# Mamba-2 scan of a trunk kernel: one masked 256x256 matrix per head instead of chunk products with a carried state

## The chip, the cores and the metric

The kernel runs on one core of a Trainium2 chip. The metric is the device time of one execution, in microseconds (us). The engines are named as the profile names them: PE (TensorE, its weight loads apart as PEld), DVE (VectorE), ACT (ScalarE), POOL (GpSimd) and SP (SyncE, which issues the transfers).

## The reference, cut to what matters

Two layers of a decoder trunk on 256 tokens of width 1024. Each layer is a gated FFN, a mixer and a second FFN; the mixer of the first layer is latent attention, that of the second is a Mamba-2 SSD block. Six sublayers follow each other, numbered s = 0 to 5; the SSD block is s = 4. Only its scan and the gate behind it are touched. With 32 heads of 64 columns, 4 groups of 8 heads, a state of 128 and two chunks of 128 tokens, the scan is

```python
a_cum = jnp.cumsum(a, axis=-1)                                   # a = dt * A, in each chunk
decay_ls = jnp.exp(jnp.where(causal, a_cum[l] - a_cum[s], -inf))
cb = einsum('bclgn,bcsgn->bcgls', Cc, Bc)
y_diag = einsum('bcgls,bcgkls,bcsgkp->bclgkp', cb, decay_ls, xdt)
states = einsum('bclgn,bcgkl,bclgkp->bcgkpn', Bc, exp(a_cum[-1] - a_cum), xdt)
# prev: the state that is carried from chunk 0 into chunk 1 (zero for chunk 0)
y_off = einsum('bclgn,bcgkpn,bcgkl->bclgkp', Cc, prev, exp(a_cum))
y = y_diag + y_off + d_skip * xs
g = rms_norm over each group of 512 columns of (y * silu(z))     # then g @ w_out
```

With two chunks the carried state can be left out: the part of chunk 1 that comes from chunk 0 is C B^T times exp(sum of a from s to l), a third 128x128 block per head beside the two causal ones on the diagonal. Both forms give the same y.

## The kernel before

Everything is kept transposed: channels on the partitions, the 256 tokens along the free axis. A weight matrix comes from DRAM in pieces of [128, 1024]; each is split into a float32r part (`whi`, a cast on ACT, line 197) and its rest (`wlo`, a subtraction on DVE, line 198), and a product is three float32r passes over them (`mm3`, line 282). One [128 x 1024] by [1024 x 256] projection is 24 such passes and is called PROJ here. Split pieces lie in `W_BUFS` = 5 buffers, and `piece` (line 222) asks for two pieces ahead.

`ssd` (line 1237) runs 41 projections in the order of `SSD_ORDER`: c is a chunk of the convolved channels (B, C and four of x for each group), z one of the gate. Between them it calls `step` (line 1243), which advances two lines of generators by one `yield` each: the scans (`ssd_dt`, then `ssd_group` for the groups 0 to 3) and the gates (`gate`, one for each group, which may run only when the group's scan has ended). There is one step ahead of a projection and one behind it, so two steps lie together between two projections. What a step issues on PE is pinned (line 271): it stays behind what was traced ahead of it. The Tile scheduler places the rest by program order and readiness.

`ssd_group` (line 1115) has 14 parts. For a group it makes, in this order: the products of B and C for the two chunks, and a transpose of B (`cbp`, lines 1171 to 1175); eight transposes that bring x to tokens by channels (`xs_tok`), scaled by dt on DVE (`xs_dt`, line 1135); four times, for two heads each, `decay` (line 1138), a bank with the cumulated decays of the two heads, spread over the partitions by two float32r products with 64 rows, and four bfloat16 products that add the causal mask; `decay_exp` (line 1150), four ACT exponentials; `times_cb` (line 1158), one DVE product with C B^T; and `ymm` (line 1163), four float32 products whose stationary operand is the masked matrix and whose moving operand is 64 columns of x. Beside these stand the state (`xe`, `sp`, `st`), its product with C (`off`), the scaling and the sum on DVE (`yt`), eight transposes back to channels by tokens (`tp`) and four DVE instructions that add the skip term (line 1232).

`gate` (line 1302) multiplies by silu(z) on DVE, squares on ACT, adds the four squares on POOL (line 1313), and leaves the reciprocal root (`rstd_cols`: four PE records of one column, a DVE scaling, a POOL power) for `spread` on PE; then DVE scales (line 1324) and the result is split for the products with w_out. `down` (line 440) makes these: the first `SSD_EARLY` = 4 chunks of the output take their first 12 of 16 terms early, in blocks of 4 terms (12 passes), with one hook behind each block: the last evacuation, 11 steps, and one that runs what is left. The last four terms of those chunks need the gate of group 3. A weight piece holds 8 terms, so an early chunk's second piece stays in its buffer until those last terms are made.

## Time and profile before

| | us |
|---|---|
| median of three runs | 1114.9 |
| lowest and highest of them | 1113.39 and 1115.18 |
| span of the profiled execution | 1112.1 |
| PE busy in it | 1087.2 (98%) |
| DVE busy | 865.9 (78%) |
| ACT busy | 613.1 (55%) |
| POOL busy | 55.1 (5%) |

The profiled execution's span goes from its first to its last instruction; the 2.8 us between it and the median are taken as what lies around it. Times in rows are us from the start of the span, durations in the grouped views ns. A float32 product of the program shows as two PE records, a float32r or bfloat16 product as one, a transpose as one. Records on PE overlap (a product's fill and drain lie beside its neighbours), so what a product costs is read from the distance between starts.

### The profile page before, as it was taken

Reading aid. Unit: us, or ns where it says so; the run is one execution under the profiler, and the core shown is the slowest. Engines: PE = TensorE matmul, PEld = TensorE weight load, DVE = VectorE, ACT = ScalarE, POOL = GpSimd, SP = SyncE. Lnnn points to the kernel's source line nnn. Section 1 sums busy time; section 2 is a strip of 40 time slices with the busy share of each in tenths; the row PEclk is TensorE's granted clock in tenths of the full one; section 3 lists DMA queues with packets and bytes.
Section 4 is the critical chain, followed back from the end, with each engine's and each line's share of the span. In section 5 each row is a group of like instructions: output and inputs, shape, how many; then the busy total and the mean of one; then the engine's idle time right before and its main releaser. Section 6 shows DMA issues by size and latency. Waiting matters only on the chain.

```text
span 1112.1 us, 21992 instructions
## 1 busy us (share of the span) xinstructions
PE 1087.2 (98%) x8950; PEld 1068.5 (96%) x8950; DVE 865.9 (78%) x1534; ACT 613.1 (55%) x1081; POOL 55.1 (5%) x108
## 2 busy tenths in 40 slices
PE   4999999999999999999999999999999899999998
PEld 3999999998999999999999999999999899999998
DVE  5889899789779878766998885697877677766642
ACT  3555444468667544444754444597678456544431
POOL 3000020010000000000000000000200300000000
PEclk9999999999999999999999999999999999999999
DMA  8888998754156888775799995444324254666630
GB/s 346 344 331 323 348 357 319 257 207 163 39 189 229 311 299 302 276 267 204 250 359 347 342 332 196 175 156 148 114 96 152 79 211 169 225 228 228 232 128 20
DMA packets 37401, 258.56 MB, mean 232 GB/s; under 512 B 4274, under 2 KB 5426, under 8 KB 6708
## 3 DMA queue, kind: packets, MB, share of 16 engines
q1 hardware_dynamic: 37300, 257.16, 63.4%
q8 instruction: 70, 1.15, 0.4%
q14 instruction: 31, 0.25, 0.1%
HBM read 256.10 MB, written 1.05 MB: 231 GB/s over the span
## 4 chain that ended last, share of the span: by engine, by line
PE 94%; DVE 2%; DMA 1%; ACT 1%; issue 1%; POOL 1%; SPq 0%; POOLq 0%; ACTq 0%; DVEq 0%
PE bank L272 92%; PE bank L277 2%; DMA raw<-in_adaw_dram 1%; DVE raw L236 1%; DVE wlo L198 0%; POOL t L1313 0%; DVE sl L307 0%; ACT whi L197 0%; ACT t L892 0%; DVE sl L1324 0%; SPq L328 0%; POOL sl L557 0%; POOL rr L415 0%; DVE sl L1232 0%; DVE sl L1306 0%
## 5 line engine op out<-in xcount | busy, mean ns | idle before, releaser
L272 PE MATMUL bank<-sl,whi 128*128 128x256 f32 (+1 forms) x5312 | 954.5, 283 | 4.5 <-ACT whi L197 4.4
L272 PEld LDWEIGHTS bank<-sl,whi 128*128 128x128 f32 x5312 | 816.3, 189 | 7.5 <-ACT whi L197 4.7
L272 PE MATMUL bank<-sl,wlo 128*128 128x256 f32 (+1 forms) x2656 | 747.7, 282 | 6.3 <-DVE wlo L198 6.3
L197 ACT CAST whi<-raw 128x1024 fp32r<-128x1024 f32 (+1 forms) x342 | 354.4, 1040 | 358.1 <-PE bank L272 251.9
L272 PEld LDWEIGHTS bank<-sl,wlo 128*128 128x128 f32 x2656 | 502.8, 189 | 7.0 <-DVE wlo L198 6.8
L198 DVE TENSOR_TENSOR wlo<-raw,whi 128x1024 fp32r<-128x1024 f32 (+1 forms) x342 | 413.4, 1213 | 108.8 <-ACT whi L197 107.0
L236 DVE SCALAR_TENSOR_TENSOR raw<-raw,cb 128x1024 f32<-128x1024 f32 x144 | 174.7, 1225 | 35.8 <-DMA raw<-in_adaw_dram 35.6
L306 ACT CAST sl<-t 128x256 fp32r<-128x256 f32 x125 | 49.0, 402 | 22.2 <-DVE t L490 16.7
L307 DVE TENSOR_TENSOR sl<-t,sl 128x256 fp32r<-128x256 f32 x125 | 51.6, 419 | 0.6 <-ACT sl L306 0.5
L272 PE MATMUL bank<-sl,sl 128*128 128x64 f32 (+4 forms) x272 | 44.0, 301 | 0.0
L435 DVE SCALAR_TENSOR_TENSOR x<-bank,mod,x 128x256 f32<-128x256 f32 x48 | 23.0, 481 | 24.4 <-PE bank L272 24.4
L490 DVE TENSOR_TENSOR t<-t,bank 128x256 f32<-128x256 f32 x70 | 29.3, 418 | 12.6 <-PE bank L272 12.6
L272 PEld LDWEIGHTS bank<-sl,sl 128*128 128x128 f32 (+1 forms) x272 | 35.1, 191 | 2.8 <-issue 1.0
L1032 DVE SCALAR_TENSOR_TENSOR sl<-t,cst,sl 128x256 f32<-128x256 f32 x72 | 35.9, 500 | 1.1 <-ACT sl L1030 0.5
L385 ACT ACTIVATE sl<-x,scol 128x256 fp32r<-128x256 f32 x40 | 20.3, 508 | 29.7 <-DVE x L435 29.6
L384 POOL CAST sl<-bspl 128x4 fp32r<-128x4 f32 x40 | 17.1, 472 | 302.5 <-DVE bspl L258 232.5
L415 POOL TENSOR_TENSOR rr<-rv,mhalf 128x2 f32<-128x2 f32 x12 | 12.4, 1033 | 305.5 <-DVE rv L411 290.5
L489 ACT ACTIVATE t<-bank 128x256 f32<-128x256 f32 x70 | 26.3, 377 | 0.0
L272 PE MATMUL bank<-whi,sl 128*128 128x384 f32 (+1 forms) x80 | 24.4, 369 | 0.0
L386 DVE SCALAR_TENSOR_TENSOR sl<-x,scol,sl 128x256 fp32r<-128x256 f32 x40 | 19.2, 482 | 4.8 <-ACT sl L385 4.8
L398 ACT ACTIVATE t<-t,mod,scol 128x256 f32<-128x256 f32 x32 | 18.3, 595 | 4.6 <-DVE t L397 4.6
L1154 ACT ACTIVATE sl<-bank,nac 128x128 f32<-128x128 f32 x64 | 18.2, 370 | 2.7 <-PE bank L272 2.3
(204 smaller groups left out, 621.4 us busy)
## 6 DMA issues: line engine op xcount, KB each, us to landing
raw<-in_wgu_dram SPq DMA_DIRECT2D x88, 1024.0 KB, 5.9
raw<-in_adaw_dram SPq DMA_DIRECT2D x72, 1024.0 KB, 6.9
raw<-in_wdn_dram SPq DMA_DIRECT2D x44, 1024.0 KB, 6.9
raw<-in_win_dram SPq DMA_DIRECT2D x19, 1024.0 KB, 4.8
raw<-in_wout_dram SPq DMA_DIRECT2D x8, 1024.0 KB, 4.8
raw<-in_mwo_dram SPq DMA_DIRECT2D x4, 1024.0 KB, 4.8
raw<-in_mwq_dram SPq DMA_DIRECT2D x3, 768.0 KB, 4.2
raw<-in_mwa_dram SPq DMA_DIRECT2D x2, 1024.0 KB, 4.8
```

The lines of the kernel that those rows point to most:

```text
L197: self.nc.scalar.copy(out=hi, in_=raw)
L198: self.nc.vector.tensor_tensor(out=lo, in0=raw, in1=hi.bitcast(F32), op=ALU.subtract)
L236: nc.vector.scalar_tensor_tensor(out=w, in0=w, scalar=1.0, in1=self.cb, op0=ALU.mult, op1=ALU.mult, accum_out=self.mod[:, q, 2 * u + i:2 * ...
L272: ins = self.nc.tensor.matmul(*a, **k)
L277: ins = self.nc.tensor.transpose(*a, **k)
L306: self.nc.scalar.copy(out=hi, in_=src)
L307: self.nc.vector.tensor_tensor(out=lo, in0=src, in1=hi.bitcast(F32), op=ALU.subtract)
L385: nc.scalar.activation(out=hi[:, 0:T], in_=self.x[m], func=AF.Copy, scale=sc)
L435: nc.vector.scalar_tensor_tensor(out=self.x[m], in0=ps[:, 0:T], scalar=self.mod[:, q, m:m + 1], in1=self.x[m], op0=ALU.mult, op1=ALU.add)
L489: nc.scalar.activation(out=tg, in_=pg[:, 0:T], func=AF.Silu)
L490: nc.vector.tensor_tensor(out=tg, in0=tg, in1=pu[:, 0:T], op=ALU.mult)
L1032: nc.vector.scalar_tensor_tensor(out=dst, in0=u[:, t:t + T], scalar=cw[:, t:t + 1], in1=dst, op0=ALU.mult, op1=ALU.add)
```

## The change

For each pair of heads the matrix gets three blocks instead of two: chunk 0, chunk 1, and chunk 1 from chunk 0. The two diagonal ones are made on DVE (add the negative cumulated decay, minimum with zero, so that no mask is needed ahead of the exponential), the third directly by ACT from the bank; one ACT exponential covers the two diagonal blocks of both heads. The mask is now on C B^T, by two POOL selections a group. `ymm` has x as the stationary operand, 64 columns wide, and the matrix as the moving one, 256 columns for chunk 0 and 128 for chunk 1; the two heads' outputs lie in the two halves of the partitions of one bank, transposed already. So the state, its product, the transposes back, the sums on DVE and the mask products go. The picking product takes all 128 rows (the lower ones zero). The generator has 11 parts instead of 14. The gate of group 3 adds its squares on DVE, `SSD_EARLY` is 5, `SSD_HOOKS` 13, and the general buffers `NSLOT` are 32 where they were 35. Comments and docstrings that went are left out of the diff.

```diff
--- before.py
+++ after.py
@@ -26,7 +26,7 @@
 RAW_BUFS = 5
 W_BUFS = 5
 AHEAD = 2
-NSLOT = 35
+NSLOT = 32
@@ -34,9 +34,9 @@
 SSD_ORDER = "ccccczzcz" + "ccczccczz" + "ccczcccz" * 2 + "zzzzzz"
 SSD_STEPS = (1, 1)
-SSD_EARLY = 4
+SSD_EARLY = 5
 SSD_EVERY = 4
-SSD_HOOKS = 11
+SSD_HOOKS = 13
...
@@ -1007,13 +1007,10 @@
         nc.vector.tensor_copy(out=self.tri, in_=u)
         self.onesr = self.const([128, 128], "s_onesr", F32R)
         self.order(nc.vector.tensor_copy(out=self.onesr, in_=self.ones))
-        m0 = self.t1()[:, 0:128]
-        self.order(nc.gpsimd.memset(m0, 0.0))
-        nc.gpsimd.affine_select(out=m0, in_=m0, pattern=[[1, 128]], compare_op=ALU.is_ge, fill=BIG_NEG, base=0,
-                                channel_multiplier=-1)
-        self.maskl = self.const([128, 128], "maskl", BF16)
-        nc.vector.tensor_copy(out=self.maskl, in_=m0)
         self.pick = self.const([128, 32], "s_pick", F32R)
+        nc.gpsimd.memset(self.pick[64:128].bitcast(F32), 0.0)
+        self.acr = self.const([128, T], "acr", F32R)
+        nc.gpsimd.memset(self.acr[64:128].bitcast(F32), 0.0)
         self.order(nc.vector.tensor_tensor(out=self.pick[0:64], in0=self.ident[0:64, 0:32], in1=self.ident[0:64, 32:64], op=ALU.add))
 
     def conv_evac(self, ps, R, j, dst):
...
@@ -1103,18 +1100,14 @@
         self.nac = self.const([128, 2, 32], "nac")
         nc.vector.tensor_scalar(out=self.nac, in0=pc[:, 0:64].rearrange("p (c h) -> p c h", c=2), scalar1=-1.0,
                                 scalar2=None, op0=ALU.mult)
-        self.ein = self.const([128, 32], "ein")
-        self.order(nc.scalar.activation(out=self.ein, in_=pc[:, 32:64], func=AF.Exp))
-        self.dte = self.const([128, 32], "dte")
-        nc.vector.tensor_tensor(out=self.dte, in0=pc[:, 64:96], in1=self.nac[:, 0], op=ALU.add)
-        self.order(nc.scalar.activation(out=self.dte, in_=self.dte, func=AF.Exp))
-        self.acr = self.const([128, T], "acr", F32R)
+        self.ate = self.const([128, 32], "ate")
+        nc.vector.tensor_tensor(out=self.ate, in0=pc[:, 64:96], in1=self.nac[:, 0], op=ALU.add)
         nc.vector.tensor_copy(out=self.acr[0:64], in_=pr[0:64, 0:T])
         nc.vector.tensor_tensor(out=self.acr[32:64], in0=pr[32:64, 0:T], in1=self.acr[32:64].bitcast(F32),
                                 op=ALU.subtract)
 
     def ssd_group(self, g, BT, CT, xsT):
-        """The scan of one group of eight heads, cut into steps; a step uses what the one before it made."""
+
         nc = self.nc
 
         def hcol(t, n):
...
@@ -1139,44 +1132,57 @@
             ps = self.bank()
             for j in range(2):
                 h = 8 * g + 2 * i + j
-                self.matmul(ps[:, j * T:(j + 1) * T], self.pick[0:64, h:h + 1].broadcast_to([64, 128]),
-                                 self.acr[0:64, :], start=(j == 0), stop=False)
-            for j in range(4):
-                self.matmul(ps[:, j * 128:(j + 1) * 128], self.identb, self.maskl, start=False, stop=(j == 3))
+                self.matmul(ps[:, j * T:(j + 1) * T], self.pick[:, h:h + 1].broadcast_to([128, 128]),
+                                 self.acr, start=(j == 0), stop=(j == 1))
             return ps
 
         def decay_exp(i, ps):
-            t = self.slot()
+
+
+            t = self.p.tile([128, 2, 3, 128], F32, name=self.name("dec"), tag="dec", bufs=3)
             for j in range(2):
                 h = 8 * g + 2 * i + j
+                o = j * T + 128
+                self.order(nc.scalar.activation(out=t[:, j, 1], in_=ps[:, o:o + 128], func=AF.Exp,
+                                                bias=self.ate[:, h:h + 1]))
                 for c in range(2):
-                    o = slice(j * T + c * 128, j * T + (c + 1) * 128)
-                    self.order(nc.scalar.activation(out=t[:, o], in_=ps[:, o], func=AF.Exp,
-                                                    bias=self.nac[:, c, h:h + 1]))
+                    o = j * T + c * 128
+                    nc.vector.tensor_scalar(out=t[:, j, 2 * c], in0=ps[:, o:o + 128], scalar1=self.nac[:, c, h:h + 1],
+                                            scalar2=0.0, op0=ALU.add, op1=ALU.min)
+            self.order(nc.scalar.activation(out=t[:, :, 0:3:2], in_=t[:, :, 0:3:2], func=AF.Exp))
             return t
 
         def times_cb(t):
-            tv = t.rearrange("p (h c l) -> p h c l", h=2, c=2)
-            nc.vector.tensor_tensor(out=tv, in0=tv, in1=bc[:, 1:3, :].rearrange("p (o c) l -> p o c l", o=1)
-                                    .broadcast_to([128, 2, 2, 128]), op=ALU.mult)
+            nc.vector.tensor_tensor(out=t, in0=t, in1=bc.rearrange("p (o c l) -> p o c l", o=1, c=3)
+                                    .broadcast_to([128, 2, 3, 128]), op=ALU.mult)
 
         def ymm(i, t):
-            for j in range(2):
-                hc = slice((2 * i + j) * 64, (2 * i + j + 1) * 64)
-                for c in range(2):
-                    self.matmul(yp[c][:, hc], t[:, j * T + c * 128:j * T + (c + 1) * 128], xdt[c][:, hc],
-                                     start=True, stop=True)
+
+            ps = self.bank()
+            for c in range(2):
+                for j in range(2):
+                    hc = slice((2 * i + j) * 64, (2 * i + j + 1) * 64)
+                    self.matmul(ps[j * 64:(j + 1) * 64, c * 128:T], xdt[c][:, hc],
+                                     t[:, j, 2 * c:2 + c],
+                                     start=(c == 0), stop=(c == 1))
+            return ps
+
+        def leave(i, ps):
+            ch = 4 * g + i
+            nc.vector.scalar_tensor_tensor(out=xsT[i], in0=xsT[i], scalar=self.dsk[:, ch:ch + 1],
+                                           in1=ps[:, 0:T], op0=ALU.mult, op1=ALU.add)
 
         yield
         cbp = self.bank()
-        self.transpose(out=cbp[:, 0:128], in_=BT[:, 0:128], identity=self.ident)
-        for c in range(2):
-            self.matmul(cbp[:, (c + 1) * 128:(c + 2) * 128], BT[:, c * 128:(c + 1) * 128],
-                             CT[:, c * 128:(c + 1) * 128], start=True, stop=True)
+        self.matmul(cbp[:, 0:T], BT[:, 0:128], CT[:, 0:T], start=True, stop=True)
+        self.matmul(cbp[:, T:T + 128], BT[:, 128:256], CT[:, 128:256], start=True, stop=True)
         x0 = xs_tok(0)
         yield
-        bc = self.t3().rearrange("p (c l) -> p c l", c=3)
-        nc.scalar.copy(out=bc, in_=cbp[:, 0:384].rearrange("p (c l) -> p c l", c=3))
+        bc = self.t3()
+        nc.scalar.copy(out=bc, in_=cbp[:, 0:384])
+        for b in (0, 2):
+            nc.gpsimd.affine_select(out=bc[:, b * 128:(b + 1) * 128], in_=bc[:, b * 128:(b + 1) * 128],
+                                    pattern=[[1, 128]], compare_op=ALU.is_ge, fill=0.0, base=0, channel_multiplier=-1)
         xdt = [xs_dt(0, x0)]
         x1 = xs_tok(1)
         d0 = decay(0)
@@ -1185,54 +1191,29 @@
         xdt.append(xs_dt(1, x1))
         d1 = decay(1)
         yield
+        times_cb(m0)
         m1 = decay_exp(1, d1)
-        times_cb(m0)
-        xe = self.slot()
-        nc.vector.tensor_tensor(out=heads(xe), in0=heads(xdt[0]), in1=hcol(self.dte, 64), op=ALU.mult)
         d2 = decay(2)
         yield
+        times_cb(m1)
         m2 = decay_exp(2, d2)
-        times_cb(m1)
-        yp = [self.bank(), self.bank()]
-        ymm(0, m0)
-        sp = self.bank()
-        self.matmul(sp, bc[:, 0, :], xe, start=True, stop=True)
-        yield
-        st = self.slot()
-        nc.scalar.copy(out=st, in_=sp)
+        y0 = ymm(0, m0)
+        yield
         times_cb(m2)
-        ymm(1, m1)
+        y1 = ymm(1, m1)
         d3 = decay(3)
+        leave(0, y0)
         yield
         m3 = decay_exp(3, d3)
-        ymm(2, m2)
-        off = self.bank()
-        self.matmul(off, CT[:, 128:256], st, start=True, stop=True)
+        y2 = ymm(2, m2)
+        leave(1, y1)
         yield
         times_cb(m3)
-        yt = [self.slot(), self.slot()]
-        nc.vector.tensor_tensor(out=heads(yt[1]), in0=heads(off), in1=hcol(self.ein, 64), op=ALU.mult)
-        yield
-        ymm(3, m3)
-        yield
-        nc.scalar.copy(out=yt[0], in_=yp[0])
-        nc.vector.tensor_tensor(out=yt[1], in0=yt[1], in1=yp[1], op=ALU.add)
-        yield
-        tp = []
-        for j in range(2):
-            ps = self.bank()
-            tp.append(ps)
-            for jj in range(2):
-                for c in range(2):
-                    self.transpose(out=ps[:, jj * T + c * 128:jj * T + (c + 1) * 128],
-                                        in_=yt[c][:, (2 * j + jj) * 128:(2 * j + jj + 1) * 128], identity=self.ident)
-        yield
-        for j in range(4):
-            ch = 4 * g + j
-            nc.vector.scalar_tensor_tensor(out=xsT[j], in0=xsT[j], scalar=self.dsk[:, ch:ch + 1],
-                                           in1=tp[j // 2][:, (j % 2) * T:(j % 2 + 1) * T], op0=ALU.mult, op1=ALU.add)
-            if j == 1:
-                yield
+        leave(2, y2)
+        yield
+        y3 = ymm(3, m3)
+        yield
+        leave(3, y3)
 
     def ssd(self, s):
         nc = self.nc
...
@@ -1309,8 +1290,9 @@
                 sq = self.t1()
                 nc.scalar.activation(out=sq, in_=xs_all[4 * g + i], func=AF.Square)
                 sqs.append(sq)
+            add = nc.vector if g == 3 else nc.gpsimd
             for i in range(3):
-                nc.gpsimd.tensor_tensor(out=sqs[0], in0=sqs[0], in1=sqs[i + 1], op=ALU.add)
+                add.tensor_tensor(out=sqs[0], in0=sqs[0], in1=sqs[i + 1], op=ALU.add)
             yield
             yield
             r = self.rstd_cols(sqs[:1], 512)
```

## Rows read from the trace of the kernel before

**Rows 1.** The page: busy time of the engines, and shares of the chain that ended last.

```profile
PE 1087.2 (98%) x8950; PEld 1068.5 (96%) x8950; DVE 865.9 (78%) x1534; ACT 613.1 (55%) x1081; POOL 55.1 (5%) x108
PE 94%; DVE 2%; DMA 1%; ACT 1%; issue 1%; POOL 1%; SPq 0%; POOLq 0%; ACTq 0%; DVEq 0%
```

**Rows 2.** Waits of PE in 700 to 925: waiter, releaser, us in total, times, longest.

```profile
PE bank L272 <- POOL t L1313: 1.8, 1, 1.8
PE bank L272 <- POOL rr L415: 1.0, 1, 1.0
```

**Rows 3.** Stretches: us, busy PE, PEld, DVE, ACT, POOL, granted clock, DMA share, GB/s.

```profile
755.00:867.40 112.40, 112.11 (x910) 104.47 (x909) 87.17 (x145) 84.34 (x180) 12.18 (x20) 1.00 0.34 118
867.40:884.30 16.90, 14.07 (x106) 13.79 (x105) 9.66 (x21) 6.22 (x12) 7.50 (x13) 0.90 0.37 125
720.00:755.00 35.00, 35.00 (x295) 34.34 (x294) 34.60 (x81) 32.35 (x61) 0.50 (x5) 1.00 0.43 151
```

**Rows 4.** PE in order of time, scan of group 0: start, us, instruction.

```profile
752.08 0.27 PE L277 MATMUL bank<-ident,sl 128*128 128x128 f32 x1
752.64 1.04 PE L277 MATMUL bank<-ident,sl 128*128 128x128 f32 x8
...
757.26 0.50 PE L272 MATMUL bank<-acr,s_pick 64*128 64x256 f32 x2
757.69 0.40 PE L272 MATMUL bank<-maskl,identb 128*128 128x128 bf16 x4
758.01 0.49 PE L272 MATMUL bank<-acr,s_pick 64*128 64x256 f32 x2
...
762.41 1.08 PE L272 MATMUL bank<-sl,t 128*128 128x512 f32 x2
763.33 1.00 PE L272 MATMUL bank<-sl,sl 128*128 128x64 f32 x8
...
772.41 1.00 PE L272 MATMUL bank<-sl,sl 128*128 128x64 f32 x8
773.22 0.48 PE L272 MATMUL bank<-sl,whi 128*128 128x256 f32 x2
...
776.16 1.04 PE L277 MATMUL bank<-ident,sl 128*128 128x128 f32 x8
776.95 0.36 PE L272 MATMUL bank<-sl,whi 128*128 128x256 f32 x1
```

**Rows 5.** PE in order of time, where 32-column weights follow and precede 128-column ones.

```profile
706.08 0.28 PE L272 MATMUL bank<-sl,wlo 128*32 128x258 f32 x1
706.20 0.41 PE L272 MATMUL bank<-sl,whi 128*128 128x258 f32 x2
```

**Rows 6.** DVE groups by shape over the span: busy us, mean ns, idle before.

```profile
L198 DVE TENSOR_TENSOR wlo<-raw,whi 128x1024 fp32r<-128x1024 f32 x334 | 406.8, 1222 | 108.3 <-ACT whi L197 106.7
L1160 DVE TENSOR_TENSOR sl<-sl,t 128x512 f32<-128x512 f32 x16 | 10.9, 686 | 4.8 <-ACT sl L1154 4.8
L888 DVE TENSOR_REDUCE mx<-bank 128x1 f32<-128x128 f32 x16 | 4.5, 283 | 0.0
L1214 DVE TENSOR_TENSOR sl<-bank,ein 128x512 f32<-128x512 f32 x4 | 2.8, 688 | 7.0 <-PE bank L272 7.0
```

**Rows 7.** ACT groups by shape over the span.

```profile
L1154 ACT ACTIVATE sl<-bank,nac 128x128 f32<-128x128 f32 x64 | 18.2, 370 | 2.7 <-PE bank L272 2.3 <-POOL t L1313 0.3
L1291 ACT ACTIVATE sl<-sl 128x512 f32<-128x512 f32 x16 | 9.0, 618 | 0.0
L1218 ACT COPY sl<-bank 128x512 f32<-128x512 f32 x4 | 2.3, 582 | 0.0
```

**Rows 8.** POOL group by shape over the span: a 128x128 selection.

```profile
L1012 POOL TENSOR_SCALAR_AFFINE_SELECT t<-t 128x128 f32<-128x128 f32 x1 | 0.3, 292 | 0.1
```

**Rows 9.** All engines in order of time, gate of group 3, brackets: idle before.

```profile
874.23 1.33 ACT L1310 ACTIVATE t<-sl 128x256 f32<-128x256 f32 x4
874.79 2.36 DVE L198 TENSOR_TENSOR wlo<-raw,whi 128x1024 fp32r<-128x1024 f32 x2
875.03 4.32 POOL L1313 TENSOR_TENSOR t<-t,t 128x256 f32<-128x256 f32 x3 [5.30 <-ACT t L1310]
...
879.40 0.60 PE L272 MATMUL bank<-ones,t 128*128 128x1 f32 x4 [1.79 <-POOL t L1313]
...
881.23 0.63 PE L272 MATMUL bank<-sl,whi 128*128 128x256 f32 x2
...
881.87 0.63 PE L272 MATMUL bank<-sl,whi 128*128 128x256 f32 x2
```

**Rows 10.** ACT in order of time, a weight cast in the early blocks of down.

```profile
890.57 1.05 ACT L197 CAST whi<-raw 128x1024 fp32r<-128x1024 f32 x1 [2.58 <-issue]
```

## The prediction

> **What bounds the kernel now.** I read the page first: PE is busy 98% of the span and 94% of the chain that ended last [rows 1], so PE time is kernel time wherever PE doesn't wait. Then the waits of PE around the SSD sublayer: two of a microsecond or more, both at POOL [rows 2]. Then the stretches: in 755 to 867.4, where the four scans run, PE is busy 112.1 of 112.4 us, DVE 87.2, ACT 84.3; behind it, in 867.4 to 884.3, PE loses 2.8 us and the granted clock is 0.90 [rows 3]. So the change is costed as PE time in the scans, plus what happens at the end, minus what DVE takes back. The order of time on PE gives the prices as distances between starts [rows 4].
>
> **The scan on PE, one group, eight transposes of x left out (they stay).** Before:
> - C B^T and the transpose of B: 752.08 to 752.64, 0.56.
> - Four decays: from one to the next 757.26 to 758.01, 0.75; so 3.00. In it the two picking products take 0.43 (757.26 to 757.69), where two ordinary float32r passes of the same width take 0.24 (0.12 from 706.08 to 706.20 [rows 5]): the 64-row form costs 0.19 extra, about 0.095 for each product. The masks are the other 0.32.
> - Four `ymm`: 772.41 to 773.22, 0.81; so 3.24.
> - The state and its product with C, 512 columns each: 762.41 to 763.33, 0.92; so 1.84.
> - The transposes back: 776.16 to 776.95, 0.79.
> Together 9.43 us, over four groups 37.7.
>
> After:
> - A float32 product of 512 columns costs 0.92, so 1.8 ns a column. C B^T now streams 256 + 128 columns: 0.69, and no transpose.
> - Four decays of two full-height passes: 4 x 0.24 = 0.96. If the loss isn't the 64 rows, they stay at 0.43, +0.76 a group.
> - `ymm` for two heads streams 2 x (256 + 128) = 768 columns: 1.38, so 5.53 for four. No row shows a 64-column weight in the upper half of the array. The nearest, 32-column weights in the lower quarter, run at the ordinary 0.12, with no loss on leaving them [rows 5], so I take the columns alone. Lower end: the halves run side by side. Each head's product is two records in a row on the same half, so a record can lie only beside its neighbour of the other half; that leaves two thirds, 0.92. Upper end: each of the eight records loses the 0.095 of the 64-row products, 2.14.
> Together 7.18, over four groups 28.7. PE gains 9.0; with the ends of `ymm`, from a gain of 16.4 to a loss of 3.1.
>
> **DVE, ACT and POOL in the scan.** Removed from DVE in a group: three products over 512 columns at 0.69, 2.06 [rows 6]. `times_cb` grows from 512 to 768 columns; between 686 ns at 512 and 1222 at 1024 a column costs 1.05 ns, so 0.95 for 0.69, +1.07 for four. New are 16 instructions of 128 columns that read a bank: the nearest row is a reduction over 128 columns of a bank, 283 ns, so 4.5; the fixed part of the two products above, 0.15, is the lower end, 2.4. Net +3.6 a group (1.4 to 3.6), +14 over four. On 87.2 that makes 101 in a stretch that PE's gain shortens to 103 [rows 3]. DVE was that full before, 34.6 of 35.0 in 720 to 755, without a PE wait, but there no pinned product stood behind it. The generator is also three parts shorter, so the gate of group 0 now falls into scan 1 and DVE is denser there; `ymm` is pinned behind `times_cb`, and behind `ymm` the next projection. I charge 3 us of PE waits (0 to 8). ACT loses 16 exponentials at 0.37 and two copies at 0.58 and gains eight at 0.37 and four of 512 columns, about 0.62 [rows 7]: 1.7 less a group, off the path. The exponential now waits for DVE and DVE's product for it, inside the 3 us. The two POOL selections are 0.29 each [rows 8], up to 1.4 each if POOL is held as in the three adds of 4.32 [rows 9]. `times_cb` waits for them, and behind it DVE's weight splits; a projection of 24 passes, 2.9 us, lies between, so 0. The two memsets in the setup replace a memset, a selection and a cast: 0. Fewer general buffers against fewer tiles in them: 0. No DMA is moved.
>
> **The end of the sublayer.** Group 3's squares are ready at 875.56, but the three POOL adds take until 879.35, PE waits 1.79 for them, and then runs three passes in 0.64 (881.23 to 881.87) instead of 0.36 [rows 9]; the stretch's clock of 0.90 means that about 3.4 us ran at the lower of the two levels, 1.2 GHz, after that idle time, about 1.5 us lost. On DVE the adds are about 0.42 each (the slope above), 1.3 in all. Two weight splits hold DVE until 877.15: if the adds come behind them they end at 878.4 and 0.8 of the wait stays; between them, nothing stays. Of 3.3 I take a gain of 2. The transposes ahead of group 2's root go (counted above); its 1.0 us wait for POOL's power [rows 2] stays.
>
> The fifth early chunk: pieces 1, 3, 5, 7 stay held, so piece 8 gets a buffer only one block of 12 passes (1.4 us) ahead of its use, and piece 9 only when it is needed. A cast of 1.05 [rows 10] and a split of 1.22 [rows 6] are 2.3; if PE keeps program order that is 0.9 + 2.3 lost. The scheduler may put the last terms of chunk 0 between, and then it is 0. I take 0.5. The three more blocks add cover where PE waits for nothing now: 0.
>
> **The sum.** -9.0 - 2.0 + 3.0 + 0.5 = -7.5. The profiled execution is 1112.1 long and 2.8 lies around it, which is the median of 1114.9; 1114.9 - 7.5 = 1107.4, rounded to 1107.
>
> **The rivals.**
> - *The halves overlap* (two column halves work at once). For it: consecutive products alternate between the halves and write different partitions. Against: no row shows two products side by side. PE gains 16.4, but then DVE's 101 us stand against a stretch of 96, and I charge 6 of waits: -16.4 - 2 + 6 + 0.5 = -11.9, 1103. The Trainium skill, "TensorE: Matmul & The Clock Gate", Part 3 (packing small matmuls), says that products in different column groups run concurrently; no run here has shown it.
> - *DVE becomes the bound.* For it: the sum of 101 against 103, and waits both ways between DVE and ACT. Against: PE waited 0.3 us in all of the scans. Waits of 8.5 instead of 3: -2.0, 1113.
> - *Narrow weights lose time at each record* and the kernel gets slower. For it: the 64-row products, the only ones that use half of the array's rows, lose 0.095 each [rows 4]. Against: the 32-column weights lose nothing [rows 5]. At 2.14 a pair PE loses 3.1: +3.1 - 2 + 3 + 0.5 = +4.6, 1119.5. It decides from 1.85 a pair on, where 16 pairs eat up all that goes: (37.7 - 6.6 - 1.5) / 16. The Trainium skill, "TensorEngine Tiling (Array Packing)", Key Properties, says that a change of the tiling mode drains the engine; the 64-row rows agree, the 32-column rows don't.
> - *The early blocks stall*: the 3.2 for pieces 8 and 9 and 1.5 more at the lower clock, in place of 0.5: -3.3, 1112.
>
> **How the numbers follow.** Chances: the forecast 0.45, overlapping halves 0.22, DVE as the bound 0.17, narrow weights 0.08, stalled early blocks 0.08. About 0.2%, 2.2 us, is what a measurement of this kernel can tell from no change. Faster by more than that: the forecast, the overlap, and half to two thirds of the DVE and early cases, 0.80. Within it: the rest of those two, 0.09. Slower: narrow weights and the worst of the DVE case, 0.11. The range of 8 in 10 reaches from below the overlap, with few waits, to above DVE as the bound: 1100 to 1114. It leaves out the narrow weights and the far ends of both others.
>
> **What the changed profile would show.** Distances on PE: a decay at 0.24 and not 0.43; `ymm` of a pair at 1.38 (0.92: overlap; 2.1: loss). The mask products, the 512-column products and nine of 17 transposes a group gone. PE waits for DVE's line of `times_cb` in the stretch of scan 1: up to 3 us by the forecast, 8 if DVE bounds. New DVE instructions of 128 columns near 0.28. At the end no POOL add ahead of the last root, no clock below 1, and a small wait or none ahead of the fifth early chunk. The forecast is wrong if `ymm` costs over 1.85, if PE's waits in the scans pass 8, or if PE runs at the lower clock anywhere in the sublayer for more than 3 us.

## The result, and the profile after

The changed kernel takes 1124.34 us (median of four runs, 1122.75 to 1124.58) where the kernel before took 1114.17 beside it: a ratio of 1.0089, 95% interval 1.0076 to 1.0102. It is slower, by 0.9%, and the forecast of 1107, its range and its sign were wrong. The profiled execution took 1124.58, its span 1122.9.

The page of the changed kernel: busy time of the engines, and the chain's shares by engine. It answers [rows 1].

```profile
PE 1077.3 (96%) x8834; PEld 1057.6 (94%) x8834; DVE 878.9 (78%) x1588; ACT 616.0 (55%) x1059; POOL 47.4 (4%) x113
PE 85%; DVE 8%; ACT 4%; issue 1%; DMA 1%; POOL 0%; SPq 0%; ACTq 0%; DVEq 0%; POOLq 0%
```

PE is busy for 9.9 us less, as was meant, and the span is 10.8 longer. DVE's share of the chain went from 2% to 8%. The waits of PE in 700 to 925 say where, against the two waits of [rows 2]:

```profile
PE bank L272 <- DVE dec L1156: 20.8, 9, 3.6
PE bank L272 <- POOL rr L415: 2.0, 1, 2.0
PE bank L272 <- POOL t L1295: 0.5, 1, 0.5
```

L1156 is `times_cb`, the product of a pair's decay matrix with C B^T: nine of 16 pairs kept PE waiting, 20.8 us together, up to 3.6 us each. The stretches of the changed kernel (columns as in [rows 3]), the first as long as the four scans took before (here the last of them runs on to 877), the others inside it:

```profile
755.00:867.40 112.40, 93.24 (x713) 85.55 (x712) 89.88 (x181) 74.30 (x141) 9.70 (x25) 0.90 0.31 108
760.00:780.00 20.00, 12.19 (x86) 10.32 (x87) 14.45 (x30) 13.98 (x26) 1.47 (x2) 0.82 0.22 70
762.60:769.40 6.80, 4.34 (x21) 3.73 (x22) 5.87 (x13) 4.79 (x8) 0.00 (x0) 0.50 0.10 43
779.70:783.10 3.40, 3.40 (x18) 3.40 (x17) 1.80 (x5) 0.42 (x1) 0.89 (x6) 0.50 0.58 239
```

Before, PE was busy 112.1 of those 112.4 us; now 93.2, and the granted clock is 0.90. In 760 to 780 all three engines have room: PE 12.2 of 20 us, DVE 14.5, ACT 14.0. So PE waits for DVE while DVE itself is not full; that isn't an engine at its bound. The last two lines are stretches at the lower level of the clock, 1.2 GHz. The scans hold five of them, 23.9 us together, each begun 0.2 to 1.8 us behind the end of one of these waits; before there was one of 3.4 us, in the last gate [rows 9]. PE was busy for 19.3 of the 23.9 us, so about half of that, 9.6 us, is an estimate of what the lower clock cost. It is rather too high: weight passes of 256 columns lie 0.21 us apart there (797.77 to 798.19 for two) and 0.12 at 2.4 GHz, which would make it 8 to 9 us.

DVE and ACT on the way of the first matrix, in order of time (L1146 is the off-diagonal exponential of one head, L1150 the logs of its two diagonal blocks, L1152 the exponential over the diagonal blocks of both heads; the last line is PE):

```profile
755.25 0.37 ACT L1146 ACTIVATE dec<-bank,ate 128x128 f32<-128x128 f32 x1
756.01 1.22 DVE L198 TENSOR_TENSOR wlo<-raw,whi 128x1024 fp32r<-128x1024 f32 x1
757.54 0.60 DVE L1150 TENSOR_SCALAR dec<-bank,nac 128x128 f32<-128x128 f32 x2
758.06 1.21 DVE L198 TENSOR_TENSOR wlo<-raw,whi 128x1024 fp32r<-128x1024 f32 x1
758.17 0.37 ACT L1146 ACTIVATE dec<-bank,ate 128x128 f32<-128x128 f32 x1 [0.66 <-DVE dec L1150]
759.19 0.60 DVE L1150 TENSOR_SCALAR dec<-bank,nac 128x128 f32<-128x128 f32 x2
759.82 0.63 ACT L1152 ACTIVATE dec<-dec 128x512 f32<-128x512 f32 x1 [0.79 <-DVE dec L1150]
760.62 0.95 DVE L1156 TENSOR_TENSOR dec<-dec,t 128x768 f32<-128x768 f32 x1
761.62 0.87 PE L272 MATMUL bank<-dec,sl 128*64 128x256 f32 x8 [2.06 <-DVE dec L1156]
```

One matrix goes ACT, DVE, ACT, DVE, ACT, DVE: it changes engine five times, and at each change it stands behind what the next engine has queued, such as the weight splits of L198, 1.22 us each. From 755.25 to the start of PE's product at 761.62 it takes 6.4 us, of which its own eight instructions are 3.5. The off-diagonal block and the second diagonal block are read from the same 128 columns of the same bank, and the two engines never read the bank at the same time: ACT's second exponential begins only when DVE's first two instructions are over. The groups of ACT in 700 to 925 (busy us, mean ns, idle before) sum that up:

```profile
L1146 ACT ACTIVATE dec<-bank,ate 128x128 f32<-128x128 f32 x32 | 11.2, 363 | 12.5 <-PE bank L272 6.7 <-DVE dec L1150 5.5
...
L1152 ACT ACTIVATE dec<-dec 128x512 f32<-128x512 f32 x16 | 9.9, 628 | 7.4 <-DVE dec L1150 7.3
```

ACT stood idle 5.5 us ahead of off-diagonal exponentials, which use nothing that L1150 makes, and 7.3 ahead of the joint ones, which do.

### The profile page after: what moved, and what is told of

The parts are those of the page before. It is cut to its first block, busy times and chain, and to the rows that moved or that the text cites. A ratio compares the mean times of both kernels' runs of the same rounds, so it can differ in the third digit from the quotient of the medians.

```text
span 1122.9 us, 21781 instructions
## 1 busy us (share of the span) xinstructions
PE 1077.3 (96%) x8834; PEld 1057.6 (94%) x8834; DVE 878.9 (78%) x1588; ACT 616.0 (55%) x1059; POOL 47.4 (4%) x113
## 4 chain that ended last, share of the span: by engine, by line
PE 85%; DVE 8%; ACT 4%; issue 1%; DMA 1%; POOL 0%; SPq 0%; ACTq 0%; DVEq 0%; POOLq 0%
PE bank L272 84%; DVE wlo L198 2%; DVE sl L1029 1%; PE bank L277 1%; ACT whi L197 1%; DMA raw<-in_adaw_dram 1%; DVE dec L1150 1%; DVE dec L1156 1%; DVE raw L236 1%; ACT L1272 1%; ACT sl L1272 1%; DVE sl L307 0%; ACT L1146 0%; DVE t L397 0%; ACT t L892 0%
## 5 line engine op out<-in xcount | busy, mean ns | idle before, releaser
L198 DVE TENSOR_TENSOR wlo<-raw,whi 128x1024 fp32r<-128x1024 f32 (+1 forms) x342 | 413.1, 1212 | 109.9 <-ACT whi L197 107.9
L272 PE MATMUL bank<-dec,sl 128*64 128x256 f32 (+1 forms) x128 | 15.9, 375 | 20.8 <-DVE dec L1156 20.8
L272 PEld LDWEIGHTS bank<-dec,sl 128*64 128x64 f32 x128 | 9.1, 149 | 25.9 <-issue 16.0
L384 POOL CAST sl<-bspl 128x4 fp32r<-128x4 f32 x40 | 14.1, 395 | 307.5 <-DVE bspl L258 231.9
L272 PE MATMUL bank<-sl,sl 128*128 128x256 f32 (+2 forms) x136 | 24.2, 312 | 0.0
L398 ACT ACTIVATE t<-t,mod,scol 128x256 f32<-128x256 f32 x32 | 18.3, 596 | 4.9 <-DVE t L397 4.9
```

What stands on the lines that cost most here:

```text
L198: self.nc.vector.tensor_tensor(out=lo, in0=raw, in1=hi.bitcast(F32), op=ALU.subtract)
L272: ins = self.nc.tensor.matmul(*a, **k)
```

## The experiments

The theory: the turns (a matrix passing from ACT to DVE and back) cost the time, because ACT and DVE read one bank and so must go one after the other in the order in which the program has them. The rivals: DVE's load (13.0 us more on the page), or too short a lead of the matrices over their products. Ratios are against runs of the kernel before on the same chip; "half clock" is the time in the scans at 1.2 GHz, from the record of the granted clock. The last two columns are of the one profiled execution: the granted clock differs between executions of one kernel (its mean is 0.995 to 0.998 in the five of e9_swap), so small differences in the last column say little.

| kernel | us, median (runs) | ratio, 95% interval | PE waits for `times_cb` | half clock |
|---|---|---|---|---|
| changed kernel | 1124.3 (4) | 1.0089 [1.0076, 1.0102] | 20.8 in 9 | 23.9 |
| e1_order | 1105.9 (4) | 0.9927 [0.9913, 0.9942] | 7.7 in 7 | 10.2 |
| e2_later | 1122.8 (4) | 1.0081 [1.0066, 1.0096] | 20.7 in 6 | 20.5 |
| e3_both | 1106.6 (4) | 0.9933 [0.9918, 0.9947] | 3.0 in 2 | 6.8 |
| e4_rows128 | 1110.5 (10) | 0.9968 [0.9959, 0.9978] | none | 0 |
| e8_banks | 1103.8 (4) | 0.9909 [0.9894, 0.9924] | 2.2 in 2 | 0 |
| e5_jouter | 1106.4 (2) | 0.9933 [0.9913, 0.9953] | 7.6 in 7 | 6.8 |
| e6_early4 | 1105.6 (4) | 0.9922 [0.9906, 0.9939] | 7.6 in 7 | 10.2 |
| e7_pool | 1105.6 (4) | 0.9928 [0.9913, 0.9943] | 7.7 in 7 | 6.8 |
| e9_swap | 1106.0 (5) | 0.9924 [0.9911, 0.9936] | 7.6 in 7 | 6.8 |
| e10_swap_scan | 1106.4 (6) | 0.9932 [0.9919, 0.9945] | 7.2 in 7 | 10.2 |

**e1_order: the same instructions of the program, DVE's four ahead of ACT's two.**

```
             for j in range(2):
...
-                self.order(nc.scalar.activation(out=t[:, j, 1], in_=ps[:, o:o + 128], func=AF.Exp, ...
                 for c in range(2):
                     o = j * T + c * 128
                     nc.vector.tensor_scalar(out=t[:, j, 2 * c], in0=ps[:, o:o + 128], ...
+            for j in range(2):
...
+                self.order(nc.scalar.activation(out=t[:, j, 1], in_=ps[:, o:o + 128], func=AF.Exp, ...
```

> The changed kernel, with one edit: for a pair of heads DVE first makes all four diagonal blocks, then ACT takes both off-diagonal ones and the joint exponential; before, ACT and DVE took turns for each head. The work is the same on every engine. The theory of turns: ACT and DVE read the same bank and are kept apart there, so a matrix passes through ACT, DVE, ACT, DVE, ACT and DVE in series, each turn behind other work in its queue, and PE waits for the last. It expects PE's waits for the product with C B^T to fall from 20.8 us to under 8, the time at the lower clock from 24 us to under 10, and 1104 to 1113 us. The theory of load (DVE has too much to do in the scans): nothing is taken off DVE, so waits of 18 to 23 us and 1122 to 1126 us.

Measured: 18.5 us faster than the changed kernel (18.0 by the ratios) with the same products, exponentials and DVE instructions, as the theory expected; only the half clock, 10.2 us, lies just above its 10. ACT loads a function table ten times in the scans where it was twelve times; no run varied that alone, but two loads of 1.28 us are 2.6 us of ACT against 13.1 us of PE's waits. The rows of ACT and DVE for the first two matrices:

```profile
756.14 2.15 DVE L1147 TENSOR_SCALAR dec<-bank,nac 128x128 f32<-128x128 f32 x8
757.25 0.63 ACT L1152 ACTIVATE dec<-bank,ate 128x128 f32<-128x128 f32 x2
757.76 0.63 ACT L1154 ACTIVATE dec<-dec 128x512 f32<-128x512 f32 x1
758.28 0.62 ACT L1152 ACTIVATE dec<-bank,ate 128x128 f32<-128x128 f32 x2
758.78 0.64 ACT L1154 ACTIVATE dec<-dec 128x512 f32<-128x512 f32 x1
759.34 1.82 DVE L1158 TENSOR_TENSOR dec<-dec,t 128x768 f32<-128x768 f32 x2
```

Each matrix changes engine twice, and DVE now runs eight blocks of two matrices in a row. DVE's load is the same (878.9 us on either page), so the load rival falls.

**e2_later: the turns left, the products one or two steps later.** The pairs' products stand that much further behind their matrices, the last decay a step earlier, with four buffers for matrices in place of three (and 30 general buffers in place of 32).

```
         m2 = decay_exp(2, d2)
+        d3 = decay(3)
+        yield
+        times_cb(m2)
+        m3 = decay_exp(3, d3)
+        yield
+        times_cb(m3)
         y0 = ymm(0, m0)
         yield
-        times_cb(m2)
         y1 = ymm(1, m1)
-        d3 = decay(3)
...
```

> The changed kernel, with the turns between ACT and DVE left as they are, but the products of a pair with x one to two steps later (the last decay a step earlier, four matrices live instead of three, 30 general buffers instead of 32; still 11 parts). The theory of turns: the chain is as long, but has two more steps, 2 to 4 us, until PE needs it: waits under 8 us, 1103 to 1113 us. The theory of load: what DVE owes only moves, waits over 15 us, 1119 us or more.

Measured: nothing gained, 20.7 us of waits. The theory of turns missed here, and the result is what the load rival expected; that rival falls by e1_order and e8_banks and not by this run. The longest wait, in order of time:

```profile
767.65 1.28 ACT L1273 ACT_TABLE_LOAD   x1
768.94 2.19 ACT L1273 ACTIVATE sl<-sl 128x512 f32<-128x512 f32 x4
771.14 1.28 ACT L1146 ACT_TABLE_LOAD   x1
772.44 0.37 ACT L1146 ACTIVATE dec<-bank,ate 128x128 f32<-128x128 f32 x1
772.84 0.61 DVE L1150 TENSOR_SCALAR dec<-bank,nac 128x128 f32<-128x128 f32 x2 [0.58 <-ACT dec L1146]
774.30 0.60 DVE L1150 TENSOR_SCALAR dec<-bank,nac 128x128 f32<-128x128 f32 x2
775.56 0.64 ACT L1152 ACTIVATE dec<-dec 128x512 f32<-128x512 f32 x1
777.45 0.94 DVE L1156 TENSOR_TENSOR dec<-dec,t 128x768 f32<-128x768 f32 x1
778.54 1.09 PE L272 MATMUL bank<-dec,sl 128*64 128x256 f32 x3 [7.35 <-DVE dec L1156]
```

The lead is used up in one place: a batch of SiLUs with a table load on either side holds ACT from 767.65 to 772.42, and behind it the turns of a single matrix still take 6.1 us. So at this wait a longer lead gains nothing while a single matrix still needs its five changes of engine behind the other work; the other five waits were not followed like this.

**e3_both: both edits.**

> Both edits together. The theory of turns: PE waits under 3 us in the scans, no lower clock there, and what the change takes off PE (about 19 us by its trace: 4.7 a group) is left: 1094 to 1102 us. The theory of load: 1117 us or more.

Measured: the waits for `times_cb` fall to 3.0 as expected, but 6.8 us ran at half clock where none was expected, and the time is that of e1_order, above the 1094 to 1102 of the theory. Two waits come in that are 0.4 us or nothing in e1_order, one for a gate's additions (L1298) and one of a transpose for a batch of SiLUs (L1275):

```profile
PE bank L272 <- POOL t L1298: 2.5, 1, 2.5
PE bank L277 <- ACT sl L1275: 2.5, 1, 2.5
```

**e4_rows128: before, with the zero rows under the picking operands alone** (128 rows in place of 64 in `decay`, everything else as before).

```
-                self.matmul(ps[:, j * T:(j + 1) * T], self.pick[0:64, h:h + 1].broadcast_to([64, 128]),
-                                 self.acr[0:64, :], start=(j == 0), stop=False)
+                self.matmul(ps[:, j * T:(j + 1) * T], self.pick[:, h:h + 1].broadcast_to([128, 128]),
+                                 self.acr, start=(j == 0), stop=False)
...
```

> The kernel before, with the padding alone: the picking products take all 128 rows, the lower 64 of both operands being zero; masks and all else as before. If the 64-row form is what costs 0.19 us a decay (prediction), 16 decays give 3.0 us: 1110 to 1112 us, and the distance from the first picking product to the first mask product falls from 0.43 to 0.24 us. If the loss is that of products next to the masks, no change: 1113 to 1115 us.

Measured: -3.2 us, within its range, against 3.0 forecast from the two 64-row rows of [rows 4].

**e8_banks: the changed kernel's order and turns, but a bank for each reader.**

```
+            pb = self.bank()
+            for j in range(2):
+                h = 8 * g + 2 * i + j
+                self.matmul(pb[:, j * 128:(j + 1) * 128], self.pick[:, h:h + 1].broadcast_to([128, 128]),
+                                 self.acr[:, 128:T], start=(j == 0), stop=(j == 1))
+            return ps, pb
...
-                self.order(nc.scalar.activation(out=t[:, j, 1], in_=ps[:, o:o + 128], func=AF.Exp,
+                o = j * 128
+                self.order(nc.scalar.activation(out=t[:, j, 1], in_=ps[1][:, o:o + 128], func=AF.Exp,
...
```

> The changed kernel as it is, with ScalarE and VectorE in the changed kernel's own order, but the off-diagonal blocks of the logs made a second time (two products of 128 columns per pair of heads) into a bank of their own, which ScalarE alone reads; VectorE alone reads the first bank. It tells the shared bank from the mere order of the instructions. Theory (the turns come from the shared bank): ScalarE's off-diagonal exponentials wait no longer for VectorE's blocks (that wait, 5.5 us in 5 in the changed kernel, goes below 1), nor VectorE's blocks for them; the joint exponential still waits for both blocks. TensorE's waits for the products with C*B fall from 20.8 us to at most 10, the half-clock time from 23.9 us to at most 14; the added products cost 32 of 0.06 to 0.12 us each, 2 to 4 us. Time 1124.3 - 11 - 5 + 3 = 1111 us, between 1107 and 1115. Rival (the queues' written order and their other work make the delay, whichever bank is read): the waits stay at 18 us or more, and with the added products the time is 1125 to 1129 us.

Measured: 20.6 us faster than the changed kernel, though 32 products were added (0.17 us for two, 2.8 in all). Waits of PE in 700 to 925, and the stretch of the scans:

```profile
PE bank L272 <- DVE dec L1161: 2.2, 2, 1.5
PE bank L272 <- POOL t L1300: 1.8, 1, 1.8
PE bank L272 <- POOL rr L415: 1.1, 1, 1.1
755.00:867.40 112.40, 106.48 (x894) 98.62 (x893) 104.58 (x217) 88.31 (x170) 14.04 (x29) 1.00 0.35 118
```

The program has the instructions in the changed kernel's order, so the order alone is not the cause: the shared bank is. ACT's off-diagonal exponentials no longer wait for DVE (5.5 us in the changed kernel), nor DVE's blocks for them (1.9). No stretch of the profiled execution's scans is at the lower clock. That execution is the fastest of the four, with a mean granted clock of 0.998; the other three have 0.995 to 0.997, so some of the lower clock is left in them. DVE is now busy 104.6 of 112.4 us and PE hardly waits, so the load rival falls a second time. It went better than expected (2.2 us of waits where up to 10 were allowed, and a time below the 1107 to 1115 of the theory). This version beats both kernels: 0.9909 of before; its interval overlaps that of e1_order.

**e9_swap: no product added; each head's logs in its own bank, read crosswise** (ACT takes head `a` and DVE head `j`: head 0 while DVE does head 1, then the other way round).

```
-            ps = self.bank()
+            pss = [self.bank(), self.bank()]
...
-            for j in range(2):
+            for a, j in ((0, 1), (1, 0)):
...
```

> The changed kernel with the same products, but the logs of the two heads of a pair in two banks in place of the halves of one; ScalarE takes head 0's off-diagonal block while VectorE takes head 1's two diagonal blocks, and then they swap. No product is added (the version with the added bank paid 0.17 us for two products in each of 16 pairs, 2.8 us, and took 1103.8). Theory (the shared bank is the cause; two banks read crosswise free both engines): TensorE's waits for the products with C*B are at most 6 us against 20.8, at most 7 us at half clock, and the time is 1103.8 - 2.8 + (0 to 3) = 1101 to 1104 us. Rival (any hand-over between the two in-order engines costs, not the bank alone; here each waits once for the other): waits of 8 us or more and two to four stretches at half clock, as with VectorE's blocks first: 1104.5 to 1108 us.

Measured: the rival's case. ACT still waits for DVE's turn in six places; the waits of ACT, and of PE:

```profile
ACT dec L1145 <- DVE dec L1149: 7.6, 6, 2.6
...
PE bank L272 <- DVE dec L1155: 7.6, 7, 1.6
```

So with one hand-over in the middle of a matrix PE waits as long as in e1_order, 7.6 against 7.7 us in the scans; two small products a pair that avoid it cost 2.8.

**e5_jouter: e1_order with a pair's products in the order head 0, head 0, head 1, head 1.**

```
-            for c in range(2):
-                for j in range(2):
+            for j in range(2):
+                for c in range(2):
```

> The version with VectorE's blocks first (1105.85 us), but the four products of a pair of heads in the order head 0 block 0, head 0 block 1, head 1 block 0, head 1 block 1, so that two products that follow each other go to the same half of the bank and of the array's columns but once. It tells why a pair of heads took 0.72 to 0.80 us where 1.38 was forecast. Theory (two products of different halves run beside each other, and need to alternate for it): the pair takes 1.2 to 1.4 us, TensorE's work grows by 16 x 0.5 = 8 us, a part of which falls into the waits that there are: 1109 to 1114 us. Rival (a product into 64 columns is cheap by itself, in any order): the pair stays at 0.7 to 0.9 us, and the time within 1.5 us of 1105.9.

Measured: the time is the rival's, but its reason isn't. One pair in the trace, its records counted up to four points of time (PE in order of time; the duration runs to the end of the last record counted):

```profile
771.61 0.43 PE L272 MATMUL bank<-dec,sl 128*64 128x256 f32 x1 [0.59 <-DVE dec L1158]
771.61 0.44 PE L272 MATMUL bank<-dec,sl 128*64 128x256 f32 x2 [0.59 <-DVE dec L1158]
771.61 0.66 PE L272 MATMUL bank<-dec,sl 128*64 128x256 f32 x4 [0.59 <-DVE dec L1158]
771.61 0.88 PE L272 MATMUL bank<-dec,sl 128*64 128x256 f32 x8 [0.59 <-DVE dec L1158]
772.42 0.50 PE L272 MATMUL bank<-sl,whi 128*128 128x256 f32 x2
772.76 0.28 PE L272 MATMUL bank<-sl,wlo 128*128 128x256 f32 x1
```

Two records of 256 columns end 0.44 us after the first began, where one takes 0.43: they lie beside each other. All eight take 0.81 to the next start. So the halves do overlap, and the order doesn't matter: the first four records, all of 256 columns and so of both heads, end within 0.66 us, though the program has head 0's 128-column product ahead of head 1's first. (A merged row names the shape of its first record only; by shape, the four records that begin from 771.6 to 771.9 are all 128x256.)

**e6_early4 and e7_pool: e1_order with four early chunks and eleven hooks, or with the last gate's additions on GpSimd.**

```
-SSD_EARLY = 5
+SSD_EARLY = 4
...
-SSD_HOOKS = 13
+SSD_HOOKS = 11
... (above e6_early4, below e7_pool; both on top of e1_order's edit)
-            add = nc.vector if g == 3 else nc.gpsimd
+            add = nc.gpsimd
```

> The version with VectorE's blocks first (1105.85 us) with four early chunks of the output product and eleven hooks, as before the change, in place of five and thirteen. It prices that part of the change. Theory (the fifth early chunk costs TensorE nothing or up to 0.5 us, and the steps of scan and gates lie as far apart as in the changed kernel): 1104.8 to 1106.9 us, TensorE's waits in the scans within 3 us of 7.7. Rival (the fifth chunk gives the last group's gate room): without it TensorE waits 2 to 5 us more in the last gate, 1108 to 1111 us.

> The version with VectorE's blocks first (1105.85 us) with the three additions of squares of the last gate on GpSimd, as before the change, in place of VectorE. It prices that part of the change, which the forecast put at 2.0 us. Theory: the root of the last gate comes later by 2 to 3 us of GpSimd's pace, TensorE waits 1.5 to 2.5 us for it, 1107 to 1108.5 us. Rival (with the fifth early chunk there is enough work to cover GpSimd's additions): 1105.4 to 1106.4 us, no wait for the additions of that gate.

Measured: neither moves the time (0.3 us, well inside the intervals); e6_early4 came out as its theory had it, e7_pool as its rival. In e7_pool GpSimd makes the last gate's three additions from 862.92 on in 2.36 us, and the product for the root comes at 872.13 and doesn't wait:

```profile
862.92 2.36 POOL L1297 TENSOR_TENSOR t<-t,t 128x256 f32<-128x256 f32 x3
872.13 0.50 PE L272 MATMUL bank<-ones,t 128*128 128x1 f32 x4
```

The one wait for GpSimd's additions in it, 1.75 us at 861.20, is of group 2's gate, whose additions are on GpSimd in every version.

**e10_swap_scan: e9_swap with both of these undone.**

> The version before this one in the list (two banks read crosswise), with four early chunks and eleven hooks and the last gate's three additions on GpSimd, as before the change: only the scan is changed. In the version with VectorE's blocks first each of these parts alone moved the time by 0.3 us or less. Theory (they are worth nothing here): within 1.5 us of the version with two banks. Rival (in a scan without turns the last gate ends last, and the forecast's 2.0 us for the additions come in): 1.5 to 3 us slower, with TensorE waiting for the additions or the root of the last gate.

Measured: 0.3 us from e9_swap. Those parts of the change are worth nothing that these runs can tell.

## Why the prediction was wrong, point by point

- **PE's waits in the scans: the step that failed.** "I charge 3 us of PE waits (0 to 8)" was 20.8. The sentence behind it, "The exponential now waits for DVE and DVE's product for it, inside the 3 us", saw the last two of a matrix's five changes of engine and put them inside the 3 us without a price for what stands in the queues. It missed the others: that the off-diagonal and the diagonal blocks are read by two engines from one bank, so that ACT and DVE alternate within a matrix (e1_order, e8_banks). The kernel before had one change of engine there, four exponentials (L1154, [rows 7]) and then DVE (L1160, [rows 6]). What the runs showed in place of the 3 us: 20.8, of which the order of two engines' instructions takes away 13.1 (e1_order) and a bank for each reader 18.6 (e8_banks). The Trainium skill, "PSUM — Partial Sum Buffer", section "PSUM bank collisions raise a hardware error", has the rule: two engines may not access one bank in the same partitions at once, two readers included, so a dependency has to keep them apart. The trace agrees, by the 5.5 us for which ACT waited ahead of L1146. That rule was not weighed in the prediction.
- **The lower clock: no term in the sum for the scans.** It stood only among what would make the forecast wrong, at 3 us. 23.9 us in the scans ran at 1.2 GHz, 8 to 9.6 us lost by estimate. It comes with the waits: each of the five stretches follows one, and in the profiled execution with 2.2 us of waits (e8_banks) there is none.
- **`ymm`: right in kind for a rival, the size off in the sum.** Taken at 1.38 a pair, measured 0.80 (792.29 to 793.09), below even the 0.92 of the rival "the halves overlap": 9.3 us more gain over 16 pairs. That rival (chance 0.22) had the mechanism; its limit, that a record can lie only beside its neighbour, is refuted by e5_jouter. The rival of the narrow weights was not all wrong either: no record of a pair loses the 0.095, but the pair begins 0.21 us behind the pass ahead of it, where passes lie 0.12 apart (791.84 to 792.08 for two, then 792.29, below). That is 0.09 a pair or 1.4 us over 16, which the distance of 0.80 doesn't hold.
- **The other PE terms held.** C B^T 0.65 for 0.69; a decay 0.24 for 0.24 (four picking records from 756.10 to 756.57); the 64-row products' loss 3.2 for 3.0 (e4_rows128).

```profile
751.52 0.81 PE L272 MATMUL bank<-sl 128*128 128x256 f32 x4
752.17 1.04 PE L277 MATMUL bank<-ident,sl 128*128 128x128 f32 x8
...
756.10 0.63 PE L272 MATMUL bank<-acr,s_pick 128*128 128x256 f32 x4
756.57 0.40 PE L272 MATMUL bank<-sl,whi 128*128 128x256 f32 x2
...
791.84 0.40 PE L272 MATMUL bank<-sl,whi 128*128 128x256 f32 x2
792.08 0.28 PE L272 MATMUL bank<-sl,wlo 128*128 128x256 f32 x1
792.29 0.87 PE L272 MATMUL bank<-dec,sl 128*64 128x256 f32 x8
793.09 0.71 PE L272 MATMUL bank<-ident,rr 128*128 128x128 f32 x4
```

- **DVE's load: right, and beside the point.** +14 forecast, +13.0 on the page (a group's terms, 4.5 + 1.07 - 2.06, make 3.5 and not the 3.6 written). The new blocks cost 342 ns and not 283, `times_cb` 954 as forecast. "DVE becomes the bound" was argued with the load; e8_banks runs at a higher DVE load with a tenth of the waits.
- **The end of the sublayer: the 2.0 us didn't show.** The last gate's wait of 1.8 [rows 2, 9] is gone, but not through VectorE's additions: with them on GpSimd the root comes without a wait as well (e7_pool, and e10_swap_scan with the former hooks), because the last gate's squares come earlier: its additions begin at 862.92 in e7_pool, where they began at 875.03 before [rows 9]. Why they come earlier was not followed. In their place group 2's gate waits 0.5 for its additions, at 880.75, and 2.0 for POOL's power where it waited 1.0.
- **The fifth early chunk: nothing against it.** 0.5 forecast, no wait of PE for its pieces, -0.3 without it (e6_early4), which is too little to be told from nothing.

The sum made again with what was measured: -18.3 for PE's work (the 9.0 and the 9.3 more), +1.4 for the beginnings of the pairs, +20.8 waits, +9.6 lower clock, -0.3 for the two waits of the gates, together +13.2 beside a span that is 10.8 longer (one stretch of 3.4 us at half clock lies outside the scans in either trace). About one of the 2.4 too many is in the estimate for the clock; the rest is not explained. Had the turns not been there, the same sum gives -18.3 + 1.4 - 0.3 = -17.2, and e8_banks shows it: the span of its profiled execution is 12.1 shorter than before with 2.8 of added products and 2.2 of waits, 17.1 together. By the medians its gain is 9.8. (The 2.8 us that the forecast takes as lying around the span are 1.7 to 1.8 in every run here that has both numbers; the forecast goes by the median, so nothing hangs on it.)

What stays open: why e3_both, with 3.0 us of waits for the matrices, isn't faster than e1_order. Two new waits of 2.5 take up what it gained in the trace, but what makes them wasn't tried; and three of its four runs have a mean granted clock of 0.992 to 0.993, below the 0.995 to 0.996 of e1_order's, so more of them ran at half clock than the trace shows.

## What to carry to other kernels

When a change lets two engines prepare one tile, count how often the tile passes from one to the other, and price each pass by what stands in the next engine's queue, not by the instruction; busy shares don't show it. Look for every pair of readers of one PSUM bank: what two engines read at the same time belongs in two banks, and a small product that makes the second copy was cheap here (2.8 us against 18.6 us of waits and most of the lower clock). Two banks help only if each has one reader: read crosswise (e9_swap) they left 7.6 us of waits. If a bank has to be shared, let one engine finish with it before the other starts; that alone brought nearly as much (1105.9 against 1103.8 us, with intervals that overlap).

## What the runs showed of the hardware that was not expected

- Float32 products of 64 stationary columns into the two halves of a bank run side by side: eight records in 0.80 us, where the ordinary four for 384 columns take 0.65. It needs no alternating order, and records of the other half begin ahead of ones that the program has first (e5_jouter). The Trainium skill, "TensorE: Matmul & The Clock Gate", Part 3, says that the products start in strict program order; the records of e5_jouter differ. In the program compiled from e5_jouter's kernel PE's instructions stand in the order of the source, head 0's 128-column product ahead of head 1's first, which points to the engine and not to the translation; the trace alone doesn't tell.
- Going into the 64-column form costs 0.09 us: its first record begins 0.21 us behind the last float32r pass, where such passes lie 0.12 apart (792.08 to 792.29). On the way out, two passes take 0.34 us where 0.24 is ordinary (772.42 to 772.76, e5_jouter); behind the float32 products of the kernel before they took 0.32 (773.22 to 773.54), so there the form adds next to nothing.
- The order of six instructions a pair, on two engines that are each 80% busy or less over the span, moved this kernel by 18.5 us, 1.6%.
